# A hybrid encoder layer on one core: queries and keys are transposed as plain float32 values and split into two parts behind the transposes

## The chip, the cores and the metric

The kernel runs on one core of a Trainium2 chip. The metric is the device time of one execution in microseconds (us); a time of a kernel is the median of several executions. A core has five engines with an instruction stream of their own: TensorE (PE in the profile; PEld is its weight load), VectorE (DVE), ScalarE (ACT), GpSimd (POOL) and SyncE (SP, which here issues the DMAs). They share the on-chip memory SBUF (128 partitions); matmul results land in PSUM, a smaller memory of eight banks of 128 x 512 float32. Engines wait for one another through semaphores.

## The reference

One encoder layer over 1024 tokens of width 1024: a gated feed-forward block (FFN1), one projection into queries, keys, values and the inputs of a state-space block (SSD), attention and SSD side by side, an output projection, a second feed-forward block (FFN2) and a gated embedding. What the change touches is the way from projected queries and keys to attention scores:

```python
q, k, v, z, xs, bm, cm, dt_raw = jnp.split(u, SPLIT_POINTS, axis=-1)
qf = _rms(q.reshape(B, S, N_Q_HEADS, HEAD_DIM), q_norm[i])      # 8 heads of 64
kf = _rms(k.reshape(B, S, N_KV_HEADS, HEAD_DIM), k_norm[i])     # 2 heads of 64
qh = _apply_rope(qf, cos, sin)    # pairs (x0, x1) -> (x0 c - x1 s, x0 s + x1 c)
kh = _apply_rope(kf, cos, sin)
...
s = jnp.einsum('bqhgd,bkhd->bhgqk', qi, k) * scale
```

Four query heads share one key head. All is float32.

## The kernel before

A float32 matrix product is made of three matmuls on rounded operands: each operand is kept as a high part (the value rounded to the matmul's input type, fp32r) and a low part (the value minus the high part), and `mm3` (line 122) adds high x low, low x high and high x high. The high part is a cast on ScalarE, the low part a subtraction on VectorE (`lo`, line 87, so that every such subtraction of the kernel carries that line). PSUM is dealt out by two pools: "sm" has four buffers of one bank, "big" two of two banks. A product that wants a buffer waits until the last reader of the buffer that it gets has read it.

The program runs FFN1, the projection and the rest one after another; each engine works through its own list of instructions in the order in which the program puts them there. In the projection, after the gate's products, come eight products for queries (one for each tile of 128 tokens, 24 matmuls of 128 x 512 each; here called q0 to q7), eight for keys and values (24 of 128 x 272; k0 to k7), and the first product of the SSD's inputs, x0 (48 of 128 x 512 in two halves). These three groups are the place of the change; all their products but x0 go into "sm" buffers, x0 into a "big" one.

Behind each product the tile is worked off in these steps. Line 840: ScalarE squares it (`sq`, two buffers). Lines 842 and 843: VectorE sums the squares of each head. Line 845: GpSimd takes the power -1/2. Lines 129 to 132: VectorE refines it with four small instructions. Line 852: VectorE multiplies the tile by it; this is the last reader of the product's PSUM buffer. Lines 858 to 860, all VectorE: the rotary step, two half-wide products with a table T2 into `sq`, one full product with a table T1, one add; the result `qn` lies in SBUF. Line 895 (878 for keys): ScalarE casts it to the high part, and VectorE subtracts (line 87, `qs<-qn,qs`) for the low part; both lie side by side in `qs`. TensorE then transposes (a matmul against the identity) blocks of 128 x 128, each with the high and the low part of one head: eight for a query tile into a "big" buffer (line 901), four for a key tile into a "sm" buffer (line 884, each key head twice, with the parts in either order). One ScalarE copy each (lines 902 and 885) brings the transposed tile to `Q` and `K`, where the scores read them.

These steps are spread over the products by a small queue, `step`: the part up to the power is issued behind the tile's own product, the part from the refinement on ("back") one product later, the subtraction one later still, and the transposes ("turn") three products after the tile's own. So tile 4's turn stands behind q7, tile 5's behind k1 and so on. What is left at the end is put between x0's halves by four entries in `pend`, two of which are taken behind each half. For two of the products in this stretch VectorE and ScalarE also split weights (`blk<-raw,blk`), and behind k0 VectorE makes the keys' tables (two instructions of line 834).

Of the kernel before, what the change touches and what calls it, by code (L numbers as in the profile page):

```python
# [36 lines left out]
class Layer:  # L37
# [778 lines left out]
    def qkv_part(self, c, xT):  # L816
        nc, tc, I = self.nc, self.tc, self.I
        Q, K, V = self.qkv
        tabs = c.enter_context(tc.tile_pool(name="tabs", bufs=1))
# [8 lines left out]
        def tables(nm, scale):  # L828
            w = self.bcast(tabs, f"w_{nm}", f"{nm}n", HD)
            ws = self.bcast(tabs, f"ws_{nm}", f"{nm}ns", HD)  # L830
            T1 = tabs.tile([P, NT, HD], F32, name="T1")
# [13 lines left out]
            nc.gpsimd.tensor_tensor(out=r, in0=ss, in1=self.mhalf[:, :nh], op=ALU.pow)  # L845
            return v, nh, sq, ss, r

        def rope(v, nh, m, ss, r, nm, t):

            self.newton(r, ss, nh)  # L850
            qn = wk.tile([P, nh, HD], F32, name="qn")
            nc.vector.tensor_tensor(out=qn, in0=v, in1=r.unsqueeze(2).broadcast_to([P, nh, HD]), op=ALU.mult)
            T1, T2 = (x[:, t] for x in T[nm])
            H2 = HD // 2
            for a in range(2):
                o = slice(a * H2, (a + 1) * H2)
                i = slice((1 - a) * H2, (2 - a) * H2)
                nc.vector.tensor_tensor(out=m[:, :, o], in0=qn[:, :, i], in1=T2[:, o].unsqueeze(1).broadcast_to([P, nh, H2]), op=ALU.mult)
            nc.vector.tensor_tensor(out=qn, in0=qn, in1=T1.unsqueeze(1).broadcast_to([P, nh, HD]), op=ALU.mult)
            nc.vector.tensor_tensor(out=qn, in0=qn, in1=m, op=ALU.add)  # L860
            return qn

        NK = NKV * HD
        late = []

        def kv_front(t, ps):
            nc.vector.tensor_tensor(out=self.dt[:, t], in0=ps[:, 256:272], in1=dtb, op=ALU.add)
# [3 lines left out]
            self.lo(V[:, t, :, 1], vv, V[:, t, :, 0])  # L871
            return st

        def kv_back(t, st):

            kn = rope(*st, "k", t).unsqueeze(2).broadcast_to([P, NKV, 2, HD])
            kd = wk.tile([P, NKV, 2, 2, HD], F32R, name="qs", bufs=4)
            nc.scalar.copy(out=kd[:, :, 0], in_=kn)

            def turn():  # L880
                pt = self.pss().rearrange("p (g j t) -> p g j t", g=NKV, j=2)
                for g in range(NKV):
                    for j in range(2):
                        nc.tensor.transpose(out=pt[:, g, j], in_=kd[:, g, j].rearrange("p a d -> p (a d)").bitcast(F32), identity=self.ident)
                nc.scalar.copy(out=K[:, :, :, t * P:(t + 1) * P], in_=pt)
            late.append(turn)
            return kd[:, :, 1], kn, kd[:, :, 0]

        def q_front(t, ps):
            return norm(ps, NQ)  # L890

        def q_back(t, st):
            qs = wk.tile([P, NQ, 2, HD], F32R, name="qs", bufs=4)
            qn = rope(*st, "q", t)
            nc.scalar.copy(out=qs[:, :, 0], in_=qn)

            def turn():
                pt = self.psb().rearrange("p (h t) -> p h t", t=P)
                qv = qs.bitcast(F32)
                for hh in range(NQ):  # L900
                    nc.tensor.transpose(out=pt[:, hh], in_=qv[:, hh].rearrange("p a d -> p (a d)"), identity=self.ident)
                nc.scalar.copy(out=Q[:, :, t * P:(t + 1) * P], in_=pt)
# [1055 lines left out]
```

## Time and profile before

| | us |
|---|---|
| median of 3 executions | 1958.57 (1957.98 to 1959.1) |
| profiled execution, its own time | 1959.67 |
| its span in the profile | 1957.8 |
| TensorE busy in the span | 1931.1 |
| VectorE busy | 1525.2 |
| ScalarE busy | 880.5 |
| GpSimd busy | 416.2 |
| mean granted TensorE clock | 0.997 of full speed |
| q0 starts / k0 starts / x0 starts | 699.01 / 747.02 / 775.57 |

The profile is one execution, recorded instruction by instruction, so its span may be set against its own time: 1.87 us lie around the span. A row of a timeline gives the start, the duration, the engine, the line of the kernel, the operation with the names of the tiles it writes and reads, and in brackets how long the engine stood idle before it and what it waited for. The chain of waits is the run of pieces of work, each of which the next had to wait for, that ends with the last instruction. A window's row gives the busy time of each engine in a stretch of the span.

### The profile page before, as it was taken

How to read it: one execution, taken by the hardware profiler on the slowest of the kernel's cores; microseconds unless marked ns; L12 is line 12 of the kernel's file. 1: busy time of each engine (PE TensorE's matmuls, PEld its weight loads, DVE VectorE, ACT ScalarE, POOL GpSimd, SP SyncE). 2: the span in 40 equal slices, each digit the busy share in tenths (PEclk: the TensorE clock that was granted, in tenths of full speed). 3: DMA queues.
4: the chain of work that ended last, by engine and by line, in shares of the span. 5: the costliest groups of instructions: out<-in, count | busy, mean ns of one | idle time of the engine just before them, and what ended most of it. 6: DMA issues, size and time to landing. Idle time of an engine off the chain costs nothing.

```text
span 1957.8 us, 25643 instructions
## 1 busy us (share of the span) xinstructions
PE 1931.1 (99%) x9132; PEld 1611.0 (82%) x9132; DVE 1525.2 (78%) x2364; ACT 880.5 (45%) x1509; POOL 416.2 (21%) x310
## 2 busy tenths in 40 slices
PE   8999999999999999999999999999999999999998
PEld 7888888888888889888888788788888888888886
DVE  7977777767679658759998778997687777877698
ACT  6433333334444125538887776633333334443311
POOL 0144545430001132011221001003545440001011
PEclk9999999999999999999999999999999999999999
DMA  8434554549865102231003473253545439986122
GB/s 300 137 125 155 193 178 145 194 174 381 280 228 197 55 38 68 88 121 45 5 1 109 135 270 119 84 175 138 187 154 194 153 138 338 341 267 221 37 76 97
DMA packets 147713, 310.34 MB, mean 159 GB/s; under 512 B 18128, under 2 KB 30800, under 8 KB 147584
## 3 DMA queue, kind: packets, MB, share of 16 engines
q1 hardware_dynamic: 147584, 308.69, 44.9%
q8 instruction: 72, 1.18, 0.2%
q14 instruction: 57, 0.47, 0.1%
HBM read 217.21 MB, written 91.42 MB: 158 GB/s over the span
## 4 chain that ended last, share of the span: by engine, by line
PE 94%; DVE 3%; ACT 1%; issue 1%; DMA 1%; POOL 0%; SPq 0%; DVEq 0%; ACTq 0%
PE sm L122 59%; PE big L508 12%; PE sm L508 9%; PE big L122 3%; PE big L1151 3%; PE sm L1173 2%; PE sm L1188 1%; PE sm L1189 1%; PE sm L1262 1%; DVE nm L1158 1%; DVE conv L969 1%; PE sm L1363 0%; PE sm L1273 0%; PE big L1669 0%; PE sm L224 0%
## 5 line engine op out<-in xcount | busy, mean ns | idle before, releaser
L122 PE MATMUL sm<-xh,blk 128*128 128x512 f32 x1424 | 441.9, 391 | 0.0
L122 PEld LDWEIGHTS sm<-xh,blk 128*128 128x128 f32 x1424 | 268.7, 189 | 55.6
L122 PE MATMUL sm<-xl,blk 128*128 128x512 f32 x736 | 285.3, 391 | 3.8 <-DVE xl L87 3.8
L122 PE MATMUL sm<-blk,xl 128*128 128x512 f32 (+2 forms) x784 | 238.4, 371 | 0.2 <-ACT xn_t L1002 0.2
L122 PE MATMUL sm<-blk,xh 128*128 128x512 f32 (+2 forms) x584 | 203.2, 379 | 0.3 <-DVE accr L1456 0.2
L108 ACT CAST blk<-raw 128x512 fp32r<-128x512 f32 (+1 forms) x168 | 101.2, 611 | 216.2 <-PE sm L122 130.1
L87 DVE TENSOR_TENSOR blk<-s,blk 128x512 fp32r<-128x512 f32 x176 | 150.9, 863 | 36.8 <-ACT blk L108 35.9
L87 DVE TENSOR_TENSOR blk<-raw,blk 128x512 fp32r<-128x512 f32 (+1 forms) x168 | 144.9, 866 | 37.0 <-ACT blk L108 36.4
L108 ACT CAST blk<-s 128x512 fp32r<-128x512 f32 x172 | 105.6, 622 | 145.4 <-PE sm L122 125.4
L122 PEld LDWEIGHTS sm<-xl,blk 128*128 128x128 f32 x736 | 138.8, 189 | 32.8 <-issue 4.2
L122 PEld LDWEIGHTS sm<-blk,xl 128*128 128x128 f32 x784 | 143.0, 188 | 24.0 <-ACT xn_t L1002 0.5
L178 POOL TENSOR_TENSOR ln_k<-ln_k,mhalf 128x1 f32<-128x1 f32 x32 | 36.9, 1158 | 583.1 <-DVE ln_k L177 578.2
L508 PE MATMUL big<-xh 128*128 128x512 f32 x576 | 138.8, 390 | 0.0
L267 POOL TENSOR_TENSOR s<-raw 128x512 f32<-128x512 f32 x34 | 55.0, 1617 | 389.0 <-DVE blk L87 293.3
L87 DVE TENSOR_TENSOR xh<-blk,xh 128x1024 fp32r<-128x1024 f32 x78 | 95.3, 1222 | 47.4 <-ACT xh L454 39.7
L454 ACT CAST xl<-blk 128x1024 fp32r<-128x1024 f32 x76 | 80.1, 1054 | 113.2 <-PE sm L508 41.0
L454 ACT CAST xh<-blk 128x1024 fp32r<-128x1024 f32 x78 | 82.2, 1054 | 105.9 <-PE big L508 44.2
L122 PEld LDWEIGHTS sm<-blk,xh 128*128 128x128 f32 x584 | 109.9, 188 | 20.4 <-DVE accr L1456 0.6
L508 PEld LDWEIGHTS big<-xh 128*128 128x128 f32 x576 | 107.9, 188 | 22.2
L87 DVE TENSOR_TENSOR xl<-blk,xl 128x1024 fp32r<-128x1024 f32 x76 | 92.8, 1221 | 41.9 <-ACT xl L454 34.2
L508 PE MATMUL big<-xl 128*128 128x512 f32 x480 | 115.8, 390 | 0.0
L122 PE MATMUL sm<-xET2h,blk 128*128 128x512 f32 x352 | 108.6, 390 | 0.0
(336 smaller groups left out, 4018.0 us busy)
## 6 DMA issues: line engine op xcount, KB each, us to landing
raw<-in_wi_dram SPq DMA_DIRECT2D x81, 512.0 KB
blk<-hS SPq DMA_DIRECT2D x154, 256.0 KB
hS<-h SPq DMA_DIRECT2D x88, 256.0 KB
wr<-in_wo_dram SPq DMA_DIRECT2D x44, 512.0 KB
blk<-wT SPq DMA_DIRECT2D x88, 256.0 KB
hS<-sg SPq DMA_DIRECT2D x66, 256.0 KB
wT<-wr SPq DMA_DIRECT2D x66, 256.0 KB
blk<-in_wo_dram SPq DMA_DIRECT2D x66, 256.0 KB
```

The source lines that it names most:

```text
L87: (eng or self.nc.vector).tensor_tensor(out=out, in0=full, in1=hi.bitcast(F32), op=ALU.subtract)
L108: self.nc.scalar.copy(out=b[:, 0, :n], in_=src)
L122: self.nc.tensor.matmul(ps, lhsT=a, rhs=b, start=(i == 0), stop=(i == n - 1))
L178: nc.gpsimd.tensor_tensor(out=r, in0=v, in1=self.mhalf[:, :1], op=ALU.pow)
L267: lambda: G.tensor_tensor(out=s1, in0=a21, in1=a22, op=ALU.add),
L454: A.copy(out=b[:, :, 0], in_=r)
L508: nc.tensor.matmul(ps[q], lhsT=b[:, 0, x, cut], rhs=b[:, 1, y], start=j == i == 0, stop=j == NP - 1 and i == 2)
L969: nc.vector.scalar_tensor_tensor(out=a[:, o], in0=ps[:, o.start + d - c:o.stop + d - c], scalar=cw[:, j, tap:tap + 1], in1=a[:, o], op0=AL ...
L1151: nc.tensor.matmul(ps[:, n * 512:(n + 1) * 512], lhsT=Q[:, h, q0:q0 + P], rhs=K[:, h // 4, j, n * 512:(n + 1) * 512], start=j == 0, stop=j ...
L1158: nc.vector.tensor_reduce(out=nm, in_=ps, axis=AX.X, op=ALU.max, negate=True)
L1173: nc.tensor.transpose(out=pt[:, k], in_=pr[:, kk * P:(kk + 1) * P], identity=self.ident)
L1188: nc.tensor.matmul(po, lhsT=vw, rhs=pth[k // 4][:, k % 4], start=k == 0, stop=False)
```

## The change

The rotary result is now transposed as a plain float32 value, two heads to a block of 128 x 128, and split behind the transposes. For a query tile these are four transposes into a "sm" buffer (line 869). ScalarE then casts the high part from PSUM to `Q` in two instructions of 64 partitions x 512 (line 872), and VectorE subtracts from PSUM to `Q` in two more of the same size (line 87, now `Q<-sm,Q`). The layout of `Q` and `K`, and the values in them, are the same as before. The key tiles are gathered four at a time in `kn`; four transposes at once turn both heads of four tiles, two casts and two subtractions of 64 x 512 split them, and two ScalarE copies (line 903) bring the parts to the other half of the partitions. The product with T1 goes to GpSimd for queries (line 858, `G`), and stays on VectorE for keys. In the queue the turns of tiles 5, 6 and 7 stand behind k0, k1 and k2 (before: k1, k2 and k3), and the two key turns behind k5's product and behind x0.

```diff
-        def rope(v, nh, m, ss, r, nm, t):
+        def rope(qn, v, nh, m, ss, r, nm, t, G):
...
-            nc.vector.tensor_tensor(out=qn, in0=qn, in1=T1.unsqueeze(1).broadcast_to([P, nh, HD]), op=ALU.mult)
+            G.tensor_tensor(out=qn, in0=qn, in1=T1.unsqueeze(1).broadcast_to([P, nh, HD]), op=ALU.mult)
             nc.vector.tensor_tensor(out=qn, in0=qn, in1=m, op=ALU.add)
...
+        def turned(blocks, hi, lo, then=None):
+            pt = self.pss()
+            for i, b in enumerate(blocks):
+                nc.tensor.transpose(out=pt[:, i * P:(i + 1) * P], in_=b, identity=self.ident)
+            src = [pt[rows[e]].rearrange("p (i t) -> p i t", t=P) for e in range(2)]
+            for e in range(2):
+                nc.scalar.copy(out=hi[e], in_=src[e])
+            def rest():
+                for e in range(2):
+                    self.lo(lo[e], src[e], hi[e])
+                if then:
+                    then()
+            los.append(rest)
...
+            h = t // 4
+            if t % 4 == 0:
+                kn[h] = wk.tile([P, 4, NKV, HD], F32, name="kn")
+            rope(kn[h][:, t % 4], *st, "k", t, nc.vector)
+            if t % 4 == 3:
+                Kv = K[:, :, :, h * 512:(h + 1) * 512]
+                hi, lo = ([Kv[rows[g], g, j].rearrange("p (i t) -> p i t", t=P) for g in range(2)] for j in range(2))
+                def then():
+                    for g in range(2):
+                        nc.scalar.copy(out=Kv[rows[1 - g], g], in_=Kv[rows[g], g].bitcast(F32))
+                late.append(lambda: turned([kn[h][:, i].rearrange("p g d -> p (g d)") for i in range(4)], hi, lo, then))
...
-            qs = wk.tile([P, NQ, 2, HD], F32R, name="qs", bufs=4)
-            qn = rope(*st, "q", t)
-            nc.scalar.copy(out=qs[:, :, 0], in_=qn)
-            def turn():
-                pt = self.psb().rearrange("p (h t) -> p h t", t=P)
-                qv = qs.bitcast(F32)
-                for hh in range(NQ):
-                    nc.tensor.transpose(out=pt[:, hh], in_=qv[:, hh].rearrange("p a d -> p (a d)"), identity=self.ident)
-                nc.scalar.copy(out=Q[:, :, t * P:(t + 1) * P], in_=pt)
-            late.append(turn)
-            return qs[:, :, 1], qn, qs[:, :, 0]
+            qn = wk.tile([P, NQ, HD], F32, name="qn", bufs=4)
+            rope(qn, *st, "q", t, nc.gpsimd)
+            Qv = Q.rearrange("p (i e) s -> p i e s", e=2)[:, :, :, t * P:(t + 1) * P]
+            hi, lo = ([Qv[rows[e ^ j], :, e] for e in range(2)] for j in range(2))
+            late.append(lambda: turned([qn[:, 2 * i:2 * i + 2].rearrange("p h d -> p (h d)") for i in range(4)], hi, lo))
...
-            if len(late) > keep or not front:
+            if len(late) > keep:
                 late.pop(0)()
...
-            step(t, ps, kv_front, kv_back, 2)
+            step(t, ps, kv_front, kv_back, 1 if t < 2 else 0)
...
-        self.pend += [lambda: step(NT, None, None, None)] * 4
+        self.pend += [lambda: backs.pop()(), lambda: None, lambda: late.pop()(), lambda: los.pop()()]
```

On TensorE, at the products k0 and k1 (the rows of 128 x 272; - is the kernel before, + the changed one):

```order
 L122 MATMUL sm<-blk,xh_5352 128x272
 L122 MATMUL sm<-blk,xl_5351 128x272
+L869 MATMUL sm<-ident,qn 128x128 x4
 L122 MATMUL sm<-blk,xl_5349 128x272
 L122 MATMUL sm<-blk,xh_5350 128x272
...
 L122 MATMUL sm<-blk,xh_5352 128x272
 L122 MATMUL sm<-blk,xl_5351 128x272
-L901 MATMUL big<-ident,qs 128x128 x8
+L869 MATMUL sm<-ident,qn 128x128 x4
```

Blocks of eight transposes into "big" have become blocks of four into "sm", and one more of them stands behind k0, so that the last query turns come one product earlier than before.

On VectorE, between the multiplication of q7 (L852 before, L851 in the change) and that of k0. Before (`T_6313` and `T_6312` are the keys' tables being made):

```order
L858 TENSOR_TENSOR sq<-qn,T_5823 128x8x32 x2
L130 TENSOR_TENSOR rs_t<-rs_t,ss 128x2
L859 TENSOR_TENSOR qn<-qn,T_5822 128x512
L834 SCALAR_TENSOR_TENSOR T_6313<-sn,ws_k 128x512
L131 TENSOR_SCALAR rs_t<-rs_t 128x2
L860 TENSOR_TENSOR qn<-qn,sq 128x512
L834 SCALAR_TENSOR_TENSOR T_6312<-cs,w_k 128x512
L132 TENSOR_TENSOR qr<-qr,rs_t 128x2
L867 TENSOR_TENSOR dt<-sm,dtb 128x16
L852 TENSOR_TENSOR qn<-sm,qr 128x128
```

The same place in the change:

```order
L87 TENSOR_TENSOR Q<-sm,Q 64x4x128
L857 TENSOR_TENSOR sq<-qn,T_5823 128x8x32 x2
L87 TENSOR_TENSOR Q<-sm,Q 64x4x128
L130 TENSOR_TENSOR rs_t<-rs_t,ss 128x2
L834 SCALAR_TENSOR_TENSOR T_6294<-sn,ws_k 128x512
L131 TENSOR_SCALAR rs_t<-rs_t 128x2
L859 TENSOR_TENSOR qn<-qn,sq 128x512
L834 SCALAR_TENSOR_TENSOR T_6293<-cs,w_k 128x512
L132 TENSOR_TENSOR qr<-qr,rs_t 128x2
L882 TENSOR_TENSOR dt<-sm,dtb 128x16
L842 TENSOR_REDUCE ss<-sq 128x2
L87 TENSOR_TENSOR V<-sm,V 128x2x64
```

Before k0's multiplication stand now two subtractions of a query turn and two instructions of k1 (L842, and L87 into V); the product with T1 is gone from here.

On GpSimd in this stretch, before:

```order
L845 TENSOR_TENSOR qr<-ss,mhalf 128x8 x8
L845 TENSOR_TENSOR qr<-ss,mhalf 128x2 x8
```

and in the change, from the power of tile 4 on (L858 is the product with T1):

```order
L845 TENSOR_TENSOR qr<-ss,mhalf 128x8
L858 TENSOR_TENSOR qn<-qn,T_5822 128x512
L845 TENSOR_TENSOR qr<-ss,mhalf 128x8 x2
L858 TENSOR_TENSOR qn<-qn,T_5822 128x512 x2
L845 TENSOR_TENSOR qr<-ss,mhalf 128x8
L845 TENSOR_TENSOR qr<-ss,mhalf 128x2
L858 TENSOR_TENSOR qn<-qn,T_5822 128x512
L845 TENSOR_TENSOR qr<-ss,mhalf 128x2 x7
```

For the first tiles each power is followed by the tile's product with T1; from tile 5 on the order is power 5, power 6, product 5, product 6, power 7, k0's power, product 7. Outside this stretch the lists keep their order but for some 15 instructions of VectorE and ScalarE at the start of FFN2's hidden products (from 1266 us on), which change places by about one instruction of 128 x 512.

More of the change, by code (lines that the diff above doesn't have):

```diff
@@ L858, in rope @@
                 nc.vector.tensor_tensor(out=m[:, :, o], in0=qn[:, :, i], in1=T2[:, o].unsqueeze(1).broadcast_to([P, nh, H2]), op=ALU.mult)
-            nc.vector.tensor_tensor(out=qn, in0=qn, in1=T1.unsqueeze(1).broadcast_to([P, nh, HD]), op=ALU.mult)
+            G.tensor_tensor(out=qn, in0=qn, in1=T1.unsqueeze(1).broadcast_to([P, nh, HD]), op=ALU.mult)
             nc.vector.tensor_tensor(out=qn, in0=qn, in1=m, op=ALU.add)
-            return qn
         NK = NKV * HD
-        late = []
+        late, backs, los = [], [], []
+        rows = [slice(r * HD, (r + 1) * HD) for r in range(2)]
+        def turned(blocks, hi, lo, then=None):
[11 more added lines that the diff above has]
+            los.append(rest)
         def kv_front(t, ps):
@@ L872, in kv_front @@
             return st
+        kn = {}
         def kv_back(t, st):
-            kn = rope(*st, "k", t).unsqueeze(2).broadcast_to([P, NKV, 2, HD])
-            kd = wk.tile([P, NKV, 2, 2, HD], F32R, name="qs", bufs=4)
-            nc.scalar.copy(out=kd[:, :, 0], in_=kn)
-            def turn():
[L881 to L885, printed above, removed]
-            late.append(turn)
-            return kd[:, :, 1], kn, kd[:, :, 0]
+            h = t // 4
[9 more added lines that the diff above has]
+                late.append(lambda: turned([kn[h][:, i].rearrange("p g d -> p (g d)") for i in range(4)], hi, lo, then))
         def q_front(t, ps):
@@ L892, in q_back @@
         def q_back(t, st):
-            qs = wk.tile([P, NQ, 2, HD], F32R, name="qs", bufs=4)
-            qn = rope(*st, "q", t)
-            nc.scalar.copy(out=qs[:, :, 0], in_=qn)
-            def turn():
-                pt = self.psb().rearrange("p (h t) -> p h t", t=P)
-                qv = qs.bitcast(F32)
-                for hh in range(NQ):
-                    nc.tensor.transpose(out=pt[:, hh], in_=qv[:, hh].rearrange("p a d -> p (a d)"), identity=self.ident)
-                nc.scalar.copy(out=Q[:, :, t * P:(t + 1) * P], in_=pt)
-            late.append(turn)
-            return qs[:, :, 1], qn, qs[:, :, 0]
-        backs, los = [], []
+            qn = wk.tile([P, NQ, HD], F32, name="qn", bufs=4)
[3 more added lines that the diff above has]
+            late.append(lambda: turned([qn[:, 2 * i:2 * i + 2].rearrange("p h d -> p (h d)") for i in range(4)], hi, lo))
         def step(t, ps, front, back, keep=1):
-            if len(late) > keep or not front:
+            if len(late) > keep:
                 late.pop(0)()
-            st = front(t, ps) if front else None
+            st = front(t, ps)
             if los:
-                self.lo(*los.pop())
+                los.pop()()
             if backs:
-                los.append(backs.pop()())
-            if front:
-                backs.append(lambda: back(t, st))
+                backs.pop()()
+            backs.append(lambda: back(t, st))
         tables("q", HD ** -0.5)
```

1 line of the change is left out of this document (removed).

## The prediction

> **What bounds the kernel now.** I read the page's head first (spans, busy times, and the shares of the chain of waits), then the chain of waits around the change.
>
> ```profile
> span 1957.8 us, 25643 instructions
> ...
> PE 1931.1 (99%) x9132; PEld 1611.0 (82%) x9132; DVE 1525.2 (78%) x2364; ACT 880.5 (45%) x1509; POOL 416.2 (21%) x310
> ...
> PE 94%; DVE 3%; ACT 1%; issue 1%; DMA 1%; POOL 0%; SPq 0%; DVEq 0%; ACTq 0%
> ```
>
> ```profile
> 739.82 0.87 PE big L901 x8
> 740.69 5.46 PE sm L122 x24
> 746.15 0.87 PE big L901 x8
> 747.02 6.08 PE sm L122 x48
> 753.11 0.87 PE big L901 x8
> 753.98 3.02 PE sm L122 x24
> 757.00 0.87 PE big L901 x8
> 757.87 3.01 PE sm L122 x24
> ...
> 764.76 0.44 PE sm L884 x4
> ...
> 775.57 5.47 PE big L122 x24
> ```
>
> TensorE is busy 99% of the span and carries 94% of the chain. In the stretch of the change (columns: start, duration, what) the pieces follow one another without a hole: q7 from 740.69, k0 and k1 from 747.02, k2 from 753.98, k3 from 757.87, x0 from 775.57, and the transposes between them at their full price. So a transpose removed is worth its time, if nothing else becomes late. What could is shown by the windows of this stretch (us; busy PE, PEld, DVE, ACT, POOL; clock; DMA share; GB/s):
>
> ```profile
> 720.00:740.00 20.00, 20.00 (x104) 16.81 (x103) 16.15 (x42) 6.79 (x10) 6.18 (x3) 1.00 0.00 1
> 740.00:753.00 13.00, 13.00 (x88) 12.01 (x87) 10.75 (x28) 7.97 (x16) 5.06 (x2) 1.00 0.40 125
> 753.00:764.00 11.00, 11.00 (x93) 11.00 (x92) 10.37 (x48) 5.07 (x11) 2.11 (x3) 1.00 0.06 23
> ```
>
> VectorE is busy 16.15 of 20.00 us, then 10.75 of 13.00, then 10.37 of 11.00: with TensorE as it is, only 2.9 us are free in the last 24. That is less than the change takes out of TensorE here, so the question is what VectorE has to do between q7 and k3.
>
> **TensorE's part.** The 0.87 us of a query turn become 0.44 (the row of four), eight times: 8 x 0.43 = 3.4, with rounding 3.5 us. Eight key turns of 0.44 become two: 2.6. In all 6.1 us. Behind x0's start lie before four key turns (1.75), after one (0.44): 1.3 us of the saving are inside x0, 4.8 ahead of it. If TensorE waited for nothing, q7 would end at 746.15 - 4 x 0.435 = 744.4 (four turns lie ahead of it), k2 would start at 744.4 + 0.44 + 3.04 + 0.44 + 3.04 + 0.44 = 751.8, k3 at 755.2, x0 at 770.8.
>
> **VectorE's part.** Now what TensorE would wait for. k2 needs a PSUM buffer, and by the program's waits it gets q7's, free behind q7's multiplication; k3 gets k0's. Before, k3 had q7's, with 3.2 us to spare: the turns now also take "sm" buffers, so each product waits for a reader one tile younger.
>
> ```profile
> 740.75 0.68 DVE L842 TENSOR_REDUCE ss<-sq 128x8 f32<-128x512 f32 x1
> ...
> 747.72 0.68 DVE L842 TENSOR_REDUCE ss<-sq 128x8 f32<-128x512 f32 x1
> 748.31 0.68 DVE L859 TENSOR_TENSOR qn<-qn,T 128x512 f32<-128x512 f32 x1
> ...
> 752.41 0.17 DVE L129 TENSOR_TENSOR rs_t<-qr 128x8 f32<-128x8 f32 x1 [1.45 <-POOL qr L845]
> 752.49 0.69 DVE L87 TENSOR_TENSOR qs<-qn,qs 128x512 fp32r<-128x512 f32 x1
> ...
> 753.37 0.28 DVE L87 TENSOR_TENSOR V<-sm,V 128x128 fp32r<-128x128 f32 x1
> ...
> 753.96 0.69 DVE L852 TENSOR_TENSOR qn<-sm,qr 128x512 f32<-128x512 f32 x1
> ...
> 754.72 0.76 DVE L858 TENSOR_TENSOR sq<-qn,T 128x256 f32<-128x256 f32 x2
> ...
> 758.18 0.29 DVE L852 TENSOR_TENSOR qn<-sm,qr 128x128 f32<-128x128 f32 x1
> ```
>
> Before, q7's sum (L842) starts at 747.72, q7's multiplication at 753.96, k0's at 758.18: 10.46 us, of which 1.45 were a wait for the power: 9.0 of work. An instruction of 512 elements lasts 0.69 and lets the next one start 0.60 later, one of 128 0.29 and 0.20. In the changed order this same stretch loses the T1 products of q6 and q7 and one low part (3 x 0.60 = 1.8) and gains four subtractions of 64 x 512 out of PSUM, the half-wide pair of q6 (0.68) and two small ones of k1 (0.4). For the subtraction out of PSUM I take the one of this kernel that has the size and reads PSUM:
>
> ```profile
> L87 DVE TENSOR_TENSOR xl<-sm,xh 128x512 fp32r<-128x512 f32 x8 | 5.5, 686 | 0.0
> ```
>
> 686 ns, so half the partitions are no cheaper if the elements per partition set the time (128x128 takes 0.28, which speaks for it): 4 x 0.60 = 2.4. If a half-width instruction cost half, it would be 1.2; I take 2.4. Sum: 9.0 - 1.8 + 2.4 + 0.7 + 0.4 = 10.7, plus waits.
>
> Where this stretch starts: q7's squares use the buffer that q5's add frees, so they can't come earlier than VectorE. I count its list with the same steps from q6's sum (740.75 before, less the 1.3 us of three shorter turns: 739.4). Up to q5's add lie this sum and q5's multiplication (1.2), two subtractions (1.2), q5's half-wide pair (0.7), four weight splits of 272 (1.4) and small ones (0.4): 744.3. The add (0.6), two more splits (0.7), q6's multiplication and two subtractions (1.8) and small ones (0.3) follow: 747.7, the same as before. TensorE's lead is used up here.
>
> ```profile
> L87 DVE TENSOR_TENSOR blk<-raw,blk 128x272 fp32r<-128x272 f32 x6 | 2.5, 439 | 0.6 <-ACT blk L108 0.6
> ```
>
> (That is the row for the splits of 272: 0.44, with the next one 0.35 later.)
>
> **GpSimd's part.** Its price is not in this stretch's rows; the nearest are additions of this size elsewhere, and the powers here:
>
> ```profile
> 309.24 1.63 POOL L268 TENSOR_TENSOR s<-s,raw 128x512 f32<-128x512 f32 x1
> 311.50 1.31 POOL L269 TENSOR_TENSOR s<-raw 128x512 f32<-128x512 f32 x1 [0.63 <-DVE blk L87]
> ...
> 742.18 1.85 POOL L845 TENSOR_TENSOR qr<-ss,mhalf 128x8 f32<-128x8 f32 x1 [4.48 <-DVE ss L843]
> 749.16 3.21 POOL L845 TENSOR_TENSOR qr<-ss,mhalf 128x8 f32<-128x8 f32 x1 [5.13 <-DVE ss L843]
> ```
>
> ```profile
> 309.64 1.78 DVE L87 TENSOR_TENSOR blk<-s,blk 128x512 fp32r<-128x512 f32 x1
> 311.35 0.67 DVE L378 TENSOR_TENSOR u<-sg,sm 128x512 f32<-128x512 f32 x1
> 311.94 1.42 DVE L87 TENSOR_TENSOR blk<-raw,blk 128x512 fp32r<-128x512 f32 x1
> ```
>
> A T1 product costs 1.31 to 1.63 us, twice VectorE's 0.69, but in a place with room: from 720 to 740 GpSimd works 6 us in 20, and eight products add 10.5 to 13 in 55. In steady state VectorE has 0.60 less for each query tile (T1 gone) and 0.60 more (two subtractions instead of one), so q0 to q5 lose nothing. Two things are not free. q7's power stands behind q6's product: product 6 starts behind the half-wide pair of q6, 1.3 us behind q7's sum, ends 1.3 to 1.6 later, and the power takes 1.85 to 3.21 more: it is ready 4.5 to 6.1 us behind the start of the stretch, where VectorE comes for it after 4.6: a wait of 0 to 1.5, I take 0.8. And the second fence shows VectorE beside GpSimd: a subtraction of two SBUF operands took 1.78 and 1.42 us there, against 0.69, while the one between them that reads "sm" took 0.67. The products of q5, q6 and q7 fall beside weight splits (`blk<-raw,blk`) and the key tables; nothing excludes that none overlaps (0), and at most each pushes one instruction by 0.7 to 1.1 (2.1 to 3.3 in all). I take two, 1.5.
>
> The Trainium skill (SBUF — State Buffer, "Who interferes with whom") says that VectorE's second port pair is the one GpSimd uses, and that this pair is an exclusive lock. The two fences agree in kind: 1.42 and 1.78 beside a GpSimd addition, 0.67 for the operation with a PSUM operand. That rule speaks against the move of T1. If each of the three late products kept VectorE out for its whole 1.31 to 1.63 us, they would cost 3.9 to 4.9 instead of 1.5, and the sum would come to 1961.4 to 1962.4; the second rival has more.
>
> **The sum.** k0's multiplication starts at 747.7 + 10.7 + 0.8 + 1.5 = 760.7 and ends 0.3 later; with 0.2 for the hand-over to TensorE (my estimate: ScalarE took q7 0.10 us behind its last matmul, 746.15 to the row below) k3 starts near 761.2, where TensorE alone would have been at 755.2 and the kernel before at 757.87.
>
> ```profile
> 746.25 0.60 ACT L840 ACTIVATE sq<-sm 128x512 f32<-128x512 f32 x1 [0.22 <-PE sm L122]
> ```
>
> ```profile
> 761.33 0.28 DVE L842 TENSOR_REDUCE ss<-sq 128x2 f32<-128x128 f32 x1
> ...
> 764.38 0.28 DVE L842 TENSOR_REDUCE ss<-sq 128x2 f32<-128x128 f32 x1
> ```
>
> From k3 on VectorE catches up: between the sums of k3 and k4 it needed 3.05 us with the key's low part of 256 (0.34), which now comes once for four tiles, so about 2.7, and TensorE needs 3.02. From k3 to x0 lie five products and one turn, 5 x 3.02 + 0.44 = 15.5, and about 0.5 at the key turn, which needs k3's add: x0 starts at 777.2, against 775.57, 1.6 later; x0 itself is 1.3 shorter. So the net is +0.3: 6.1 us of transposes turn into waits of TensorE at k2, at k3 and around the turns between. FFN2's start has some 15 instructions in another order, each displaced by one of 0.60:
>
> ```profile
> 1267.95 0.68 DVE L388 TENSOR_TENSOR sg<-u,sm 128x512 f32<-128x512 f32 x1
> 1268.55 0.69 DVE L268 TENSOR_TENSOR s<-s,raw 128x512 f32<-128x512 f32 x1
> ```
>
> VectorE is back to back there, so 0 to 0.6 may show; I take 0.1. ScalarE is no bound: one copy of 1.02 us (the group below) and a cast become two casts of 64 x 512, and it works 7.97 of 13 us.
>
> ```profile
> L902 ACT CAST Q<-big 128x1024 fp32r<-128x1024 f32 x8 | 8.1, 1017 | 4.2 <-PE big L901 4.2
> ```
>
> The profiled execution took 1959.67, 1.87 of it around the span; with 0.4 more it is 1960.1. It lies 1.1 us above the median of 1958.57, so I predict 1959.0.
>
> The likeliest case's own range: with no collision and a power of 1.85, k3 starts at 758.9 (-2.0); with three collisions of 1.1 and the power at 3.21, at 763.7 (+2.8). Against the median that is 1956.5 to 1961.5.
>
> **Rivals.** All go by one number, the start of k3, T: net = T - 760.9 (16.0 to x0, less 1.3, against 775.57).
>
> First, TensorE keeps its bound and the saving stays. For it: 94% of the chain, and VectorE has lost eight T1 products. It needs VectorE to have q7's and k0's multiplications done by 751.8 and 755.2, so 4 to 5 us earlier than the sum says; that comes if the stretch starts early (q5's add and q7's squares by 744.5 instead of 746) and the subtractions cost half. Then T = 755.2, net -5.7: 1952.9. Against it: VectorE's 10.37 of 11.00 us.
>
> Second, slower: GpSimd's T1 and VectorE lock each other out through the chain q5's add, q7's squares, q7's power, q7's multiplication. Each of the three products then pushes two VectorE instructions by 0.73 (1.42 - 0.69) to 1.09 (1.78 - 0.69), 4.4 to 6.5, where I took 1.5; T = 764.1 to 766.2, net +3.2 to +5.3, and where the power goes to 3.21 too, 0.7 more: 1963.2 as its middle. It decides from T = 764.8 on. For it: power 7 took 3.21 where others took 1.85. Against it: in the stretch four of VectorE's instructions of this size now read PSUM.
>
> Third, the waits move but the end does not feel them: some later wait is set by a DMA or by x0's chain, and takes up either sign. Against it: what follows x0 starts from x0's end on TensorE. It gives 1958.6, within the forecast's range, and only its cause would differ.
>
> **Chances.** The forecast (with the third) 0.65, TensorE keeping the saving 0.18, slower by collisions 0.17. What this measurement can tell from no change is 0.2%, 3.9 us: faster means below 1954.65, slower above 1962.5. Of the first rival 0.14 lies beyond it (the rest keeps part of the saving), and 0.02 of the forecast's edge: faster 0.16. Of the second 0.14, and 0.04 of the forecast: slower 0.18. Same 0.66. The range goes from 1953.8 to 1963.4, and leaves out about 0.1 on each side.
>
> **What would show it.** In the profile of the changed kernel: 40 transposes and blocks of 0.44; q7's end about 1.5 us earlier; waits of TensorE ahead of k2 (2 to 4 us) and k3 (1 to 3) put down to VectorE's L851; k3's start near 761.2; from k4 on no wait over 0.5; x1 within 2 us of before. The subtractions `Q<-sm,Q` at 0.69; T1 on GpSimd at 1.3 to 1.6. No waits at k2 and k3 would make the forecast wrong on the fast side; T1 above 2 us, or `blk<-raw,blk` above 1.4 beside it, on the slow side.

## The result, and the profile after

The changed kernel takes 1962.93 us (median of 9, 1961.1 to 1964.17) against 1958.57 (median of 9, 1957.25 to 1960.25): a ratio of 1.0022, 95% interval 1.0013 to 1.0030. It is slower by 4.4 us, 0.22%. Its profiled execution took 1962.0 with a span of 1960.2 us, 2.3 us more than the profiled one before; e8 below shows that two executions of one program can differ by nearly as much.

The page's head of the changed kernel (spans, busy times, shares of the chain):

```profile
span 1960.2 us, 25545 instructions
...
PE 1928.4 (98%) x9076; PEld 1605.8 (82%) x9076; DVE 1530.4 (78%) x2360; ACT 875.4 (45%) x1500; POOL 426.1 (22%) x318
...
PE 91%; DVE 5%; ACT 1%; issue 1%; POOL 1%; DMA 1%; SPq 0%; DVEq 0%; ACTq 0%
```

The 56 transposes are gone (9132 instructions of TensorE have become 9076). TensorE's share of the chain of waits has dropped from 94% to 91%, VectorE's has gone from 3% to 5%. The waits of TensorE from the first query product to the SSD's first products (tile that waits, what it waited for, us in total, times, longest):

```profile
PE sm L869 <- DVE qn L859: 2.7, 1, 2.7
PE sm L122 <- DVE Q L87: 0.9, 1, 0.9
PE sm L122 <- DVE qn L851: 0.8, 1, 0.8
PE sm L869 <- DVE kn L859: 0.6, 1, 0.6
PE sm L122 <- DVE kn L851: 0.4, 1, 0.4
```

Before, there was no hole here. Now tile 6's turn waits 2.7 us for tile 6's add, k1 0.9 for tile 4's subtractions, k2 0.8 for q7's multiplication, the first key turn 0.6, k3 0.4 for k0's multiplication: unrounded, 5.3 us in all. And that is not all. Windows of 2 us (us; busy PE, PEld, DVE, ACT, POOL; granted clock; DMA share; GB/s):

```profile
754.00:756.00 2.00, 0.00 (x0) 0.00 (x0) 1.92 (x5) 0.00 (x0) 1.64 (x1) 1.00 0.40 129
756.00:758.00 2.00, 0.96 (x4) 0.58 (x4) 1.90 (x10) 1.04 (x4) 0.65 (x1) 0.63 0.33 133
758.00:760.00 2.00, 1.88 (x8) 1.88 (x9) 1.63 (x5) 0.55 (x1) 0.05 (x1) 0.50 0.00 0
760.00:762.00 2.00, 2.00 (x11) 2.00 (x10) 1.94 (x4) 0.00 (x0) 1.28 (x1) 0.50 0.00 0
762.00:764.00 2.00, 2.00 (x13) 1.93 (x12) 1.66 (x7) 0.43 (x2) 0.00 (x0) 0.66 0.00 0
764.00:766.00 2.00, 1.58 (x13) 1.41 (x12) 1.55 (x7) 1.16 (x2) 0.70 (x1) 1.00 0.00 0
```

Behind the hole of 2.7 us the granted clock falls to 0.50 for 6.8 us (1.5 + 2 + 2 + 1.4, from the four values below 1). In the chain of waits of the changed kernel the 24 products of k2 show it:

```profile
699.73 10.91 PE sm L122 x48
...
758.12 5.62 PE sm L122 x24
...
781.11 10.91 PE big L122 x48
...
817.44 10.91 PE big L122 x48
```

5.62 us where they took 3.02 before. x0 starts at 781.11, 81.38 us after q0 (699.73); before it was 76.56 (775.57 - 699.01). In the rows `817.44` here and `813.23` before stands the first product of the SSD's inputs behind the first turns of line 1001 (line 1007 in the change); I call it the mark.

```profile
813.23 10.91 PE big L122 x48
```

From q0 it is 117.71 us after, 114.22 before: **3.5 us later**. Stages are compared from q0 on, because q0 itself was 0.72 us apart in the two executions, ahead of everything that was changed. How VectorE spent the stretch (start, duration, line, operation), and GpSimd beside it:

```profile
740.26 0.69 DVE L842 TENSOR_REDUCE ss<-sq 128x8 f32<-128x512 f32 x1
...
744.23 2.22 DVE L87 TENSOR_TENSOR blk<-raw,blk 128x272 fp32r<-128x272 f32 x3
...
746.64 0.68 DVE L859 TENSOR_TENSOR qn<-qn,sq 128x512 f32<-128x512 f32 x1
...
748.94 1.39 DVE L87 TENSOR_TENSOR Q<-sm,Q 64x512 fp32r<-64x512 f32 x2
750.36 0.69 DVE L842 TENSOR_REDUCE ss<-sq 128x8 f32<-128x512 f32 x1
...
752.44 1.58 DVE L87 TENSOR_TENSOR blk<-raw,blk 128x512 fp32r<-128x512 f32 x1
...
758.58 0.69 DVE L87 TENSOR_TENSOR Q<-sm,Q 64x512 fp32r<-64x512 f32 x1 [0.34 <-ACT Q L872]
...
760.80 0.68 DVE L130 TENSOR_TENSOR rs_t<-rs_t,ss 128x2 f32<-128x2 f32 x1
...
763.77 0.17 DVE L882 TENSOR_TENSOR dt<-sm,dtb 128x16 f32<-128x16 f32 x1 [0.34 <-PE sm L122]
...
764.25 0.28 DVE L851 TENSOR_TENSOR kn<-sm,qr 128x128 f32<-128x128 f32 x1
```

```profile
744.45 1.34 POOL L858 TENSOR_TENSOR qn<-qn,T 128x512 f32<-128x512 f32 x1 [0.99 <-DVE sq L857]
751.86 1.61 POOL L858 TENSOR_TENSOR qn<-qn,T 128x512 f32<-128x512 f32 x1 [6.06 <-DVE sq L857]
```

From q6's sum (740.26) to tile 6's subtractions (758.58) VectorE waits for nothing, and k0's multiplication, which k3 needs, comes at 764.25. Two instructions of 64 x 512 take 1.39 us: 0.70 each. The three splits of 272 that began at 744.23 took 2.22 us beside the T1 product of tile 5 (744.45 to 745.79), and the split at 752.44 1.58 instead of 0.69 beside that of tile 6 (751.86 to 753.47).

### The profile page after: what moved, and what is told of

It reads as the page before. It is cut to its first block, busy times and chain, and to the rows that moved or that the text cites. A ratio compares the mean times of both kernels' runs of the same rounds, so it can differ in the third digit from the quotient of the medians.

```text
span 1960.2 us, 25545 instructions
## 1 busy us (share of the span) xinstructions
PE 1928.4 (98%) x9076; PEld 1605.8 (82%) x9076; DVE 1530.4 (78%) x2360; ACT 875.4 (45%) x1500; POOL 426.1 (22%) x318
## 4 chain that ended last, share of the span: by engine, by line
PE 91%; DVE 5%; ACT 1%; issue 1%; POOL 1%; DMA 1%; SPq 0%; DVEq 0%; ACTq 0%
PE sm L122 56%; PE big L508 12%; PE sm L508 9%; PE big L122 3%; PE big L1157 3%; PE sm L1179 2%; PE sm L1194 1%; PE sm L1195 1%; POOL qr L845 1%; PE sm L1268 1%; DVE nm L1164 1%; DVE conv L975 0%; DVE Q L87 0%; PE big L224 0%; PE sm L224 0%
## 5 line engine op out<-in xcount | busy, mean ns | idle before, releaser
L87 DVE TENSOR_TENSOR blk<-s,blk 128x512 fp32r<-128x512 f32 x176 | 151.1, 863 | 33.7 <-ACT blk L108 32.9
L87 DVE TENSOR_TENSOR blk<-raw,blk 128x512 fp32r<-128x512 f32 (+1 forms) x168 | 148.8, 891 | 31.8 <-ACT blk L108 31.4
L87 DVE TENSOR_TENSOR xh<-blk,xh 128x1024 fp32r<-128x1024 f32 x78 | 95.1, 1220 | 48.4 <-ACT xh L454 42.3
L87 DVE TENSOR_TENSOR xl<-blk,xl 128x1024 fp32r<-128x1024 f32 x76 | 92.6, 1219 | 40.5 <-ACT xl L454 32.8
```

Of the source, the lines that this page charges most:

```text
L87: (eng or self.nc.vector).tensor_tensor(out=out, in0=full, in1=hi.bitcast(F32), op=ALU.subtract)
```

## The experiments

Theory V: VectorE's list from q5 to k0's multiplication sets when k3 starts. Against it stand theory G (the sharing of VectorE and GpSimd is the loss), theory B (the PSUM buffers that the turns now take), theory C (the low clock behind the holes), and that the key part is to blame. All times are medians, and each ratio is to runs of the kernel before on the same chip (their medians lie from 1958.32 to 1958.92); "x0" and "mark" are us after q0 in the profile.

| kernel | us (n) | ratio to before (95%) | x0 | mark, against before |
|---|---|---|---|---|
| before | 1958.57 (9) | 1 | 76.56 | 0 |
| the change | 1962.93 (9) | 1.0022 (1.0013 to 1.0030) | 81.38 | +3.5 |
| e1 T1 on VectorE | 1962.14 (11) | 1.0023 (1.0014 to 1.0032) | 80.10 | +2.3 |
| e2 turns in big | 1964.15 (10) | 1.0026 (1.0016 to 1.0035) | 81.30 | +3.4 |
| e3 filler at tile 6's turn | 1961.05 (11) | 1.0014 (1.0005 to 1.0023) | 79.86 | +2.0 |
| e4 keys only | 1958.24 (11) | 0.9998 (0.9989 to 1.0007) | 75.27 | -1.4 |
| e5 low parts by ScalarE | 1956.62 (11) | 0.9992 (0.9983 to 1.0000) | 74.45 | -3.4 |
| e6 queries only | 1964.72 (5) | 1.0036 (1.0024 to 1.0049) | 82.64 | +6.2 |
| e7 queries 0 to 3 | 1961.68 (11) | 1.0016 (1.0007 to 1.0025) | 76.86 | +0.2 |
| e8 before, one execution | 1957.77 (1) | - | 76.56 | 0.0 |
| e9 e4 and filler in FFN2 | 1958.66 (11) | 1.0000 (0.9991 to 1.0008) | 75.28 | -1.4 |
| e10 before and filler in FFN2 | 1959.30 (11) | 1.0004 (0.9995 to 1.0013) | 76.56 | 0.0 |
| e11 e1 and e3 | 1960.19 (11) | 1.0008 (1.0000 to 1.0017) | 81.18 | +3.3 |

**e1: the T1 product back on VectorE.**

```diff
-            rope(qn, *st, "q", t, nc.gpsimd)
+            rope(qn, *st, "q", t, nc.vector)
```

> The changed kernel with the T1 product of the queries back on VectorE (the only edit). Theory V, that VectorE's list between q5 and k0 sets when k3 starts: the list gets three products of 0.6 us back (+1.8) and loses what GpSimd's products pushed it by (in the trace of the change 2.3 us: splits of 1.35 and 1.58 us instead of 0.44 and 0.69, a table instruction 0.5 late) and the 1.5 us wait for q5's power; net 0 to -2 us against the change, so 1961 to 1963. Theory G, that the sharing of GpSimd and VectorE is the whole loss: -3.5 us or more, 1959.5 or less. Theory C, that the low TensorE clock behind the holes is the loss: it changes only as far as the holes do, and k2 stays at 5.6 us if the hole ahead of it stays above 2 us.

The splits fell back to their own length:

```profile
743.53 1.14 DVE L87 TENSOR_TENSOR blk<-raw,blk 128x272 fp32r<-128x272 f32 x3
...
751.37 0.68 DVE L87 TENSOR_TENSOR blk<-raw,blk 128x512 fp32r<-128x512 f32 x1
```

1.14 for 2.22 and 0.68 for 1.58: the push by GpSimd is real, 1.1 and 0.9 us, together 2.0. But VectorE has T1 back (three times 0.6), and k3 starts 63.7 us after q0 instead of 64.9, x0 1.3 earlier. That is Theory V's 0 to -2 us; theory G's 3.5 do not come. The total does not show the 1.3 us (1.0023 for 1.0022): the eleven executions go from 1960.61 to 1966.32 us, and the five above 1965 have a mean granted clock of 0.994 where the other six have 0.996 to 0.998.

**e2: the query turns in the big buffers.**

```diff
-            pt = self.pss()
...
+            pt = (pool or self.pss)()[:, :512]
...
-            late.append(lambda: turned([qn[:, 2 * i:2 * i + 2].rearrange("p h d -> p (h d)") for i in range(4)], hi, lo))
+            late.append(lambda: turned([qn[:, 2 * i:2 * i + 2].rearrange("p h d -> p (h d)") for i in range(4)], hi, lo, None, self.psb))
```

> The changed kernel with the query turns in the big PSUM buffers, as before the change (half of one is used). Theory B, that the turns' claim on the small buffers makes the waits: k1, k2 and k3 lose their waits of 0.9, 0.8 and 0.4 us and get q-tiles' buffers, three products of slack come back, -3.5 us or more, 1959.5 or less. Theory V: the turns of tiles 6 and 7 still wait for their tile's add on VectorE (2.7 us before tile 6's turn in the change, and tile 7's add ends near 762.8), so k3 starts near 763.4 instead of 764.6: -0.7 to -1.5 us, about 1962.

The waits for buffers are gone, and all their time is at the turns (waits of TensorE in e2):

```profile
PE big L869 <- DVE qn L859: 5.1, 2, 4.1
PE sm L869 <- DVE kn L859: 0.9, 1, 0.9
```

x0 starts at 81.30, for 81.38. Theory B falls: with buffers enough TensorE waits for the same chain of instructions on VectorE at another place. The median is no better than the change's.

**e3: the clock held up.**

```diff
+            if front is kv_front and t == 1:
+                idle = self.psb()
+                for i in range(16):
+                    nc.tensor.transpose(out=idle[:, i % 8 * P:(i % 8 + 1) * P], in_=self.ident, identity=self.ident)
             if len(late) > keep:
```

> The changed kernel with 16 transposes of the identity into an unused big buffer put ahead of tile 6's turn (1.75 us of work in a hole of 2.66; the output doesn't use them), so that TensorE idles no more than about 1 us there. Theory C: the granted clock stays at 1.0 in the 756 to 764 us windows where it was 0.5 to 0.66, k2 takes 3.0 us instead of 5.6, and the kernel gains 2.6 to 3.1 us: 1960. Theory V: the clock stays up and k2 takes 3.0, but k3 waits for k0's multiplication all the same, longer by what k2 is shorter: 0 to -0.5 us, 1962.5 to 1963.

The clock stayed at 1.00 in this stretch (window of e3):

```profile
753.00:764.00 11.00, 7.71 (x60) 6.83 (x59) 10.54 (x34) 3.19 (x8) 4.31 (x4) 1.00 0.14 48
```

k2 took its 3.0 us, and k3 started 63.6 us after q0 instead of 64.9, the mark came 1.5 us earlier. So the low clock costs 1.3 to 1.5 us, half of what theory C said and far more than the 0 to 0.5 of theory V. V had not counted that slow work on TensorE makes VectorE's own inputs late: in the change VectorE stands 0.34 us for ScalarE's cast at 758.58 and 0.34 for k2's end at 763.77, and the small instruction at 760.80 takes 0.68 beside tile 7's T1 product, where in e3 it takes 0.16. What is left with the clock up, +2.0 at the mark and 4.7 at k3 (63.6 against 58.9), is VectorE's list, with the collisions in it.

**e4 and e6: one part alone.** In e4 the queries are turned as before and only the keys are gathered by fours and split behind the turn; in e6 it is the reverse. e4 against the change, and below it e6 (the versions of before of `q_back` and `kv_back`, and the products behind which their turns stand):

```diff
-            qn = wk.tile([P, NQ, HD], F32, name="qn", bufs=4)
-            rope(qn, *st, "q", t, nc.gpsimd)
...
+            qs = wk.tile([P, NQ, 2, HD], F32R, name="qs", bufs=4)
+            qn = wk.tile([P, NQ, HD], F32, name="qn")
+            rope(qn, *st, "q", t, nc.vector)
+            nc.scalar.copy(out=qs[:, :, 0], in_=qn)
...
-            step(t, ps, kv_front, kv_back, 1 if t < 2 else 0)
+            step(t, ps, kv_front, kv_back, 2 if t < 2 else 1 if t < 3 else 0)
```

```diff
-            rope(kn[h][:, t % 4], *st, "k", t, nc.vector)
...
+            rope(kn, *st, "k", t, nc.vector)
+            kn = kn.unsqueeze(2).broadcast_to([P, NKV, 2, HD])
+            kd = wk.tile([P, NKV, 2, 2, HD], F32R, name="qs", bufs=4)
+            nc.scalar.copy(out=kd[:, :, 0], in_=kn)
...
-            step(t, ps, kv_front, kv_back, 1 if t < 2 else 0)
+            step(t, ps, kv_front, kv_back, 1 if t < 2 else 0 if t == 2 else 2)
```

> Only the key part of the change: the queries go as before (split, eight transposes into a big buffer, T1 on VectorE), the keys are gathered by fours, turned as plain values and split behind it. TensorE loses 24 transposes (2.6 us). Theory V: VectorE loses eight low parts of 0.34 us and gets four of 0.7, none of it ahead of k3, so nothing new waits: -1.8 to -2.6 us against the kernel before, 1956 to 1957, and 6 to 7 us below the change. If the key part itself makes waits (the first key turn needs k3's add, 0.6 us in the change), the gain is 2 us. A result at or above the kernel before would put the loss into the key part.

> Only the query part of the change: plain values turned and split behind it, T1 on GpSimd; the keys as before (split, four transposes for each tile). Theory V: the waits up to k3 stay as in the change, k3 starts 64 to 65 us after q0 (58.9 before), and the keys' turns give back 1.3 us ahead of x0: x0 at 82 to 83 us after q0, 1963 to 1965. If the loss came from the two parts together, the waits shrink and it is under 1961.

The key part makes no hole, and x0 starts 1.3 us earlier, what three of four key turns cost. The query part alone has all the waits and puts x0 at 82.64, as theory V said (82 to 83): the loss is the query part's, also in the median (1964.72). But e4 missed in its total: -0.5 us, not clear of no change, where 1.8 to 2.6 were expected; more on that below.

**e5: the subtractions off VectorE.** ScalarE writes the low parts of the queries as copies, and the subtraction is left out; its scores are therefore not the reference's, and it serves only for its time.

```diff
-                    self.lo(lo[e], src[e], hi[e])
+                    if then:
+                        self.lo(lo[e], src[e], hi[e])
+                    else:
+                        nc.scalar.copy(out=lo[e], in_=src[e])
```

> The changed kernel with the low parts of the queries written by ScalarE as copies of the value from PSUM (two instructions of 64 x 512 as before, so the traffic and the waits for them stay, but nothing is subtracted and VectorE doesn't do them). This takes 2 x 0.70 us for each query tile off VectorE. Theory V: of the stretch from q5's refinement to k0's multiplication (24.7 us of VectorE in the change, 20.4 before) 5.6 us go, the holes ahead of tile 6's turn, k2 and k3 close, the clock stays at 1.0, and x0 starts 72 to 74 us after q0 (81.4 in the change, 76.6 before): 6 to 8 us below the change, 1955 to 1957. If ScalarE, which gets 1.2 us more for each tile, or the T1 products on GpSimd hold the same chain, less than half of it comes: x0 at 78 or later.

```profile
PE sm L122 <- ACT Q L879: 0.6, 1, 0.6
PE sm L869 <- ACT Q L879: 0.5, 1, 0.5
PE sm L869 <- DVE kn L859: 0.5, 1, 0.5
```

Without the 1.4 us for each tile the wait of 2.7 shrinks to 0.5, and that is for ScalarE now; x0 starts 74.5 us after q0, 6.9 earlier than in the change, and the mark comes 3.4 earlier than before the change. Eight subtractions at 0.70 and the 1.3 us of the low clock, which goes with the holes, add up to these 6.9 us. This is the strongest evidence for theory V: the eight subtractions from PSUM ahead of k0's multiplication are the load that VectorE could not carry. The median is 6.3 us below the change's.

**e7: the query part for tiles 0 to 3 only**, T1 on VectorE and the turns in big buffers, and the key part; tiles 4 to 7 as before the change.

```diff
+            if t < 4:
+                rope(qn, *st, "q", t, nc.vector)
...
+                late.append(lambda: turned([qn[:, 2 * i:2 * i + 2].rearrange("p h d -> p (h d)") for i in range(4)], hi, lo, None, self.psb))
+                return
             qs = wk.tile([P, NQ, 2, HD], F32R, name="qs", bufs=3)
```

> The key part of the change for all tiles, the query part only for tiles 0 to 3 (turned as plain values into a big buffer, T1 on VectorE); tiles 4 to 7 go as before, so that ahead of k3 VectorE has no subtraction out of PSUM but tile 3's. Theory V: TensorE keeps the saving of four query turns (1.75 us) and of the first key turns (1.3), no holes, x0 73.5 us after q0 (76.6 before), clock 1.0; 2.5 to 3.5 us below the kernel before: 1955 to 1956. If VectorE is already full in the queries' steady state (5.4 us of work for a tile against 5.9 of TensorE), waits of 0.5 to 1 us show at q5 to q7 and the gain is 1 to 2 us.

A miss. The wait of TensorE in e7 at the keys' first product:

```profile
PE sm L122 <- DVE blk L87: 2.1, 1, 2.1
```

Its window of the steady state, 16.65 us of VectorE in 20:

```profile
720.00:740.00 20.00, 20.00 (x98) 16.57 (x97) 16.65 (x43) 5.17 (x10) 6.35 (x4) 1.00 0.00 0
```

And VectorE's list (q0 at 700.17):

```profile
749.42 0.68 DVE L842 TENSOR_REDUCE ss<-sq 128x8 f32<-128x512 f32 x1
...
751.04 1.03 DVE L87 TENSOR_TENSOR blk<-raw,blk 128x272 fp32r<-128x272 f32 x2
```

q7's sum came 49.25 us after q0, against 48.71 before, though TensorE had q7 ready 1.7 us earlier; the last splits of the keys' weights stand behind it, and k0 itself waited 2.1 us for them. So with T1 on VectorE even four tiles bring nothing: what TensorE is early VectorE has to be early too, in a list with little room, and the weights are next in line. But this makes only 0.3 us at x0 and 0.2 at the mark. The rest of the 3.4 us in the median is not of this place: in the profile the granted clock fell at the mark (0.70 from 816 to 820), whose product took 12.54 us for 10.91, and once more later (0.67 and 0.64 from 1100 to 1110).

**e8, e9, e10: how sure the ends are.** In FFN2, TensorE runs 1680 matmuls of line 122 behind a hole of 3.8 us; they lasted 383.87 us in the first profile of before. Once more:

> The kernel before once more, for its profile: how much the same program's stages differ between two profiled executions. In the first profile x0 started 76.56 us after q0, and FFN2's hidden products lasted 383.87 us, against 382.5 to 382.7 in the five changed kernels. If FFN2's different order is what makes that, it is 383.9 again; if it is a difference between executions, it is near 382.6.

The row of the first profile, then e8's:

```profile
1260.86 383.87 PE sm L122 x1680
...
1260.28 382.64 PE sm L122 x1680
```

382.64: the same program, 1.2 us apart. x0 and the mark stood within 0.01 us of the first profile. The other order in FFN2 therefore shows no effect. In the first profile the clock was low there for twice as long: windows of before, and of e8's execution,

```profile
1259.00:1262.00 3.00, 1.14 (x3) 0.97 (x4) 3.00 (x6) 0.48 (x1) 0.00 (x0) 0.66 0.11 14
1262.00:1265.00 3.00, 3.00 (x9) 2.33 (x8) 3.00 (x6) 2.42 (x4) 0.00 (x0) 0.50 0.94 352
1265.00:1268.00 3.00, 3.00 (x11) 2.40 (x10) 1.79 (x4) 0.52 (x1) 0.00 (x0) 0.70 0.83 324
```

```profile
1259.00:1262.00 3.00, 1.72 (x4) 1.46 (x5) 3.00 (x6) 0.03 (x1) 0.00 (x0) 0.71 0.25 52
1262.00:1265.00 3.00, 3.00 (x11) 2.36 (x11) 2.95 (x5) 2.91 (x4) 0.00 (x0) 0.72 1.00 367
1265.00:1268.00 3.00, 3.00 (x15) 2.49 (x14) 1.38 (x3) 0.00 (x0) 0.00 (x0) 1.00 0.69 273
```

about 6.8 and 3.4 us at half clock behind the same hole of 3.8 us. To fill this hole, 28 transposes of the identity were put ahead of FFN2's first product, in e4 (e9) and in the kernel before (e10):

```diff
-                p0 = first(w0)
+                p0 = first(w0, None, 28)
```

> The key part alone (as in e4) with 28 transposes of the identity into an unused big buffer ahead of FFN2's first product, where TensorE stands 3.8 us in every profile and the granted clock then is 0.5 for one or two spells of 3.4 us (the output doesn't use them). Theory C2, that what a saving ahead of the attention gains at the end is decided by such spells behind later holes: the spell at FFN2 goes, its products there run at 1.0, 1.2 to 3 us less than e4: 1955 to 1957, and below the kernel before clear of noise. If the spell costs nothing because the products there wait for VectorE anyway, it is e4's time, 1958.

> The kernel before with the same 28 transposes ahead of FFN2's first product and nothing else. Theory C2: 1.2 to 3 us below the kernel before, 1955.5 to 1957.5, and e9 another 0.5 to 1.4 us below it. If the filler delays the first product (it would end after the operands are there) the time is the same or worse.

Neither gained: 1.0000 and 1.0004, both intervals across 1. They did not test the expectation, because the transposes were not in the hole: FFN2's first product, which the expectations took for the one behind the hole, runs earlier. In e10:

```profile
1215.84 3.27 PE L1756 MATMUL big<-ident 128*128 128x128 f32 x28
...
1261.39 0.47 PE L122 MATMUL sm<-xl,blk 128*128 128x512 f32 x1 [2.37 <-DVE xl L87]
```

TensorE ran them between its products some 40 us ahead of the hole (from 1215.84, in e9 from 1218.1). They were 3 us of extra work, and a hole of 2.37 us was left; counted from q0, the first of the 1680 matmuls came 2.1 us later in e9 than in e4, and 0.9 us later in e10 than before. In e9 the clock stayed up behind the hole of 2.37 us and the 1680 matmuls took 381.06 us, 1.4 less than in e4; in e10 a low stretch of 3.4 us followed a hole of the same length.

**e11: both repairs of the query part at once**, e1 and e3.

> The changed kernel with both single repairs at once: T1 back on VectorE (e1) and 16 transposes of the identity ahead of tile 6's turn (e3). The two took 1.2 and 1.3 us off the start of k3 after q0 (64.9 in the change: 63.7 and 63.6; 58.9 before). If they are separate causes, k3 starts 62.3 to 62.6 us after q0, the later stages 2.2 to 2.6 us earlier than in the change, and the kernel is at 1960 to 1961, still above the kernel before: what is left, 3.5 us at k3, is VectorE's longer list. If they are one cause, k3 stays at 63.5 or more.

k3 starts 63.66 us after q0 (763.27 - 699.61): the two do not add. With T1 on VectorE, its own list was that long already: from q7's sum to k0's multiplication it took 13.1 us in e1, under the low clock, and 13.0 here. The fillers kept the clock up at k2, but four holes of 0.8 to 1.1 us followed one another (0.91, 0.77, 1.11 and 0.94), and a low stretch came behind them (e11, k3 and k4):

```profile
762.00:764.00 2.00, 1.06 (x6) 0.82 (x5) 1.90 (x11) 1.24 (x3) 0.70 (x1) 0.76 0.00 0
764.00:766.00 2.00, 2.00 (x11) 2.00 (x10) 1.92 (x8) 0.16 (x1) 0.00 (x0) 0.50 0.00 0
766.00:768.00 2.00, 2.00 (x16) 2.00 (x16) 0.98 (x7) 0.27 (x2) 0.00 (x0) 0.88 0.04 8
```

The median is 2.7 us better than the change's, and its interval still lies at or above the kernel before.

No kernel here beats the one before clear of noise. The key part alone (e4, e9) is better than the change by some 4 us and equal to the kernel before.

**What a saving is worth at the end.** From q0, the first of the 1680 matmuls in FFN2 stood at 561.9 before (561.2 in e8), 564.7 in the change, 561.7 in e4, 561.2 in e5. The change's 3.5 us of loss at the mark are 2.8 to 3.5 there; e4's 1.4 and e5's 3.4 us of gain are -0.5 to 0.6. Between the two lies the SSD's loop, in which TensorE waits for VectorE's state update, 4.4 us before and 3.5 to 5.6 in the other kernels; in e4 and e5 a stretch of low clock stood there that the kernel before did not have. The first row is e4, the second e3; before and in the change both windows were at 1.00:

```profile
1095.00:1100.00 5.00, 3.73 (x11) 3.08 (x12) 4.29 (x8) 5.00 (x16) 0.00 (x0) 0.66 0.26 99
...
1100.00:1105.00 5.00, 5.00 (x26) 4.32 (x25) 3.67 (x7) 5.00 (x19) 0.00 (x0) 0.66 0.08 30
```

It is not only gains that meet it. From the mark to the first of the 1680 matmuls, the profiles without such a stretch took 446.9 to 447.7 us (before, e8, the change, e1, e6, e11), and those with one near 1100 us 448.8 to 451.1 (e2, e3, e4, e5, e7), whether they were ahead of the kernel before at the mark (e4, e5) or behind it (e2, e3, e7). So the time between the two follows the clock and not the sign of what came before. That this stretch eats the gain of e4 and e5 is likely and not shown: no run took it away.

## Why the prediction was right in its range and wrong in its middle

The range, 1953.8 to 1963.4, holds the 1962.93. The middle, 1959.0, and the class were off by one step: 0.22% lies just beyond the 0.2% taken as the bound of no change. The 1962.93 also lies outside the likeliest case's own range, 1956.5 to 1961.5: what held it was the allowance for the second rival, whose mechanism the runs do not bear out, and that is luck. The mechanism of the forecast was right in kind: 6.1 us of transposes became waits of TensorE for VectorE from k1 to k3 and at the turns between. It had put 2 to 4 us of them at k2 and 1 to 3 at k3, both for L851. Most stood elsewhere: 2.7 at tile 6's turn, for L859, and 0.9 at k1, for a turn's subtractions; k2 and k3 waited 0.8 and 0.4 for L851.

By its own number T, the start of k3, counted from q0: forecast 62.2 (761.2 - 699.01), measured 64.86, 2.7 us more. The terms:

- **The start of the stretch** (q7's sum): forecast 747.7, which is 48.7 after q0; measured 750.36, 50.6: +1.9. From q6's sum to q5's add it counted 4.9 us and it took 6.4. 1.1 of this is the collision of tile 5's T1 product with the splits (2.22 against 1.14 in e1); the prediction booked all its collisions behind this point. The rest is the subtractions at 0.70 each instead of 0.60, four times before q7's sum, and small steps.
- **Its length** up to k0's multiplication: forecast 13.0 (10.7 and 0.8 and 1.5), measured 13.9; with the clock held (e3) 12.6. So the sum was right within 0.4 but for the low clock's 1.3, a term that the prediction did not have at all. In part that is luck: the 0.8 for the power of q7 measured nothing (it was ready at 755.82, and VectorE came for it at 756.36), and four subtractions at 0.70 instead of 0.60 took half of it back.
- **From k3 to x0**: forecast 16.0, measured 16.5. **x0 to the mark** 1.3 shorter, as forecast (36.3 for 37.7).

0.3 forecast, and 1.9 + 0.9 - 0.2 (hand-over) + 0.5 more, make 3.5 unrounded. The missing term could have been read off the profile of before: behind the hole of 3.8 us in FFN2 the granted clock stood at 0.50 and 0.66 to 0.70 in the three windows from 1259 to 1268 quoted above. A forecast that opens a hole of TensorE has to price what follows it. The Trainium skill ("TensorE: Matmul & The Clock Gate", "Part 1: The HAM clock gate") says that an idle window of about 3.4 us halves TensorE's clock, and that the window runs free, so that the same kernel can meet it differently. The traces agree in the length (6.8 and 3.4 us low) and in the chance (6.8 and 3.4 us behind the same hole in two executions of one program); but here a hole of 2.7 us did it, in e10 one of 2.37, and in e11 four holes of about 1 us each, so idleness need not fill the window.

The rivals. TensorE keeping the saving: no; VectorE could not, as e5 shows by taking the load off. Slower by collisions: they are real (2.0 us measured in e1 for two of the products), and the sign given for them came, a split above 1.4 (1.58). But without them, with T1 back on VectorE, x0 came only 1.3 us earlier, and the mark was still 2.3 us later than before the change; and by the rival's own number, k3's start at 764.8 or later, it did not come: 64.86 us after q0 is 763.87 on the scale of before. So the second rival had the right side and not the right cause. The third, that a later wait takes up either sign, did not happen to the loss, which reached FFN2. The gains of e4 and e5 hardly reached it, and in both profiles a stretch of low clock stood on the way. The term for FFN2's order, 0.1, measured nothing.

## What to carry to other kernels

Where TensorE is 99% busy, ask how much room the engine that feeds it has in the same microseconds: here VectorE had 2.9 us in 24, and a change that moves work to it by 0.7 us an instruction took more than TensorE saved. An instruction's time went by the elements of one partition: two subtractions of 64 x 512 cost twice one of 128 x 512, so a split behind a transpose that halves the partitions doubles its price. Price a hole in TensorE's work by its length and by the slow clock that may follow it, and compare stages from a mark ahead of the change: x0 and the mark stood within 0.01 us in two executions whose ends were 1.8 us apart. And look in the trace where an added filler ran: in e9 and e10 it ran 40 us ahead of the hole that it was meant for.

## What the runs showed of the hardware

- A hole of 2.66 us in TensorE's work (e1 2.65, e6 2.67) was followed by 6.8 us at half the granted clock; with no hole above 1.11 in its place (e3) the clock stayed at 1.00, but behind four holes of 0.8 to 1.1 us (e11) it fell for 3.4 us. Behind a hole of 3.8 us it fell for 6.8 us in one execution and for 3.4 in another of the same program, behind one of 2.37 us for 3.4 (e10) or not at all (e9).
- A VectorE split with two SBUF operands beside a GpSimd product of 1.3 to 1.6 us took 0.9 to 1.1 us longer (1.58 for 0.68, 2.22 for 1.14); subtractions that read PSUM kept 0.69 to 0.70.
- Two instructions of 64 x 512 out of PSUM, one behind the other, took 1.39 us, 0.70 each, where the prediction had taken 0.60 as the distance from a 128 x 512 instruction to the next.
